# A hybrid decoder layer: GpSimd's stores issued two steps later in the forgetting stage

## The chip, the cores and the metric

The kernel runs on one core of a Trainium2 chip. A core has TensorE (matrix products, PE in the profile), VectorE (DVE), ScalarE (ACT), GpSimd (POOL) and SyncE (SP), each with a queue of its own that it works off in order, and 16 DMA engines that all queues share. The time is microseconds on the device for one execution; less is better.

## The reference

One decoder layer with two groups of attention heads over the same input (2048 rows, width 1024).

```python
h = rms_norm(x, g_pre) * (1 + scale) + shift          # shift, scale, gate from silu(c) @ w_ada + b_ada
qa, ka, va, fa, za, qb, kb, vb, zb = split(h @ w_in)
# A, "forgetting": causal softmax attention, 8 heads of 64, with a bias cum[q] - cum[k],
#    cum = cumsum(log_sigmoid(fa + b_fgate)) over the rows
oa = forgetting_attention(qa, ka, va, fa + b_fgate) * silu(za)
# B: sliding window of 128 with sinks, 8 query heads, 2 key heads, rotary positions
ob = sliding_window_sink_attention(rope(qb), rope(kb), vb, sinks) * silu(zb)
y = concatenate([oa, ob]) @ w_out
x + gate * rms_norm(y, g_post)
```

The change touches group A's stage, in which three more things are done on the side: gate paths `silu(za)`, the projection of the next heads' queries and keys, and the vector `gate * g_post`, with `gate = silu(c) @ w_ada[:, 2048:] + b_ada[2048:]`.

## The kernel before

The order of instructions on each engine is written out by hand (`tc.manual_schedule()`), so an engine's queue follows the order in which the Python code runs. Waits between engines are set by the tiles that they share.

**Stages.** Opening and normalisation, then projections with the sliding window (to about 485 us in the profile), the forgetting stage, and the output projection. In the forgetting stage a loop runs over 160 *steps*: 8 heads of 20 steps, and step `s` is `hd, r = divmod(s, 20)`. A step takes two blocks of 128 keys against up to 512 queries:

- `scores`: TensorE writes the scores into the PSUM tile `sta` (L1248, L1249), of which there is one.
- `exp32`: ScalarE takes the exponential into `p` (L1253). In the steps on the diagonal, r = 0, 1, 4, 5, 10, 11, 18 and 19, GpSimd then applies the causal mask to `p` in place (L1257, `affine_select`).
- `high`: ScalarE copies `p` to f16 in `pha` (L1261), after the mask where there is one.
- `low`: VectorE takes the rest, `p` minus that copy (L1264), one step later.
- `pv`: TensorE multiplies both with the values (L1274 to L1277), two steps later.

So on ScalarE the next step's exponential stands behind this step's `high`, and the next scores but one can be written only when that exponential has read `sta`.

**Between them** `todo`, a list of small units, is spread over each step: one unit of a projection (L305) for the heads ahead (through `fill`), or one matmul that finds row maxima of the scores (L1199), which VectorE reduces (L1202, L1204). `events` hang a weight's preparation on the counts of these units: `w_load` loads a weight of 512 KB (L203), `w_max` reduces it on VectorE to a maximum per partition (L209) and stores that to DRAM (`mx_d`, L212), `w_back` loads all 128 of them back to every partition (`mxr`, L217), `w_scale` takes their maximum (L228) and sets the scale, `w_high` and `w_low` split the weight. All DMAs of this list are issued from GpSimd's queue, the one that applies the masks.

**Delays.** `after(n, f)` calls `f` at the n-th `tick()` from then, and there are two ticks in a step. `evac_z` takes a finished gate path out of PSUM this way: ScalarE's tanh after one tick (L349), VectorE's product after two (L345), and with it the store of the tile `tz` to `z_d` (L347, 256 KB) from GpSimd. There are two tiles `tz`.

**The residual gate.** `gate_load(k)` loads rows of `w_ada` into the one tile `gw` (512 KB, L1128, from GpSimd), for k = 0 to 9 at the end of step 8k; `gate_use(k)` accumulates them in `gacc` on VectorE (L1134) at the end of step 8k + 6.

Of the kernel before, what the change touches and what calls it, by code (L numbers as in the profile page):

```python
# [21 lines left out]
KT = D // P  # L22
# [18 lines left out]
def hybrid_layer(  # L41
# [17 lines left out]
    V, A, G, PE, SP = nc.vector, nc.scalar, nc.gpsimd, nc.tensor, nc.sync  # L59
# [20 lines left out]
    def sm(n, tag):  # L80
        return small.tile([P, n], F32, tag=tag, name=tag)
# [98 lines left out]


    late = []

    def after(n, f):
        late.append([n, f])

    def tick():
        now = [f for n, f in late if n <= 1]
        late[:] = [[n - 1, f] for n, f in late if n > 1]
        for f in now:  # L190
            f()


    wq = {}
# [12 lines left out]
    def w_max(key):  # L207
        mx = sm(1, "w_mx")
        V.tensor_reduce(mx[:], wq[key][0][:], axis=AX.XY, op=ALU.max, apply_absolute_value=True)  # L209
        md = mx_d[len(kaps_seen) % 3]  # L210
        kaps_seen.append(key)
        G.dma_start(md[:], mx[:])  # L212
        wq[key].append(md)

    def w_back(key):
        mxr = mxp.tile([P, P], F32, tag="mxr", name="mxr")
# [123 lines left out]
    def evac_z(kt, key, ci):  # L340
        def evac(ps, free):
            t = op_.tile([P, CH], F32, tag="tz", name="tz")

            def mul():
                V.scalar_tensor_tensor(t[:], t[:], 1.0, ps, op0=ALU.add, op1=ALU.mult)  # L345
                free()
                G.dma_start(z_d[kt, :, ci * CH:(ci + 1) * CH], t[:])  # L347

            after(1, lambda: A.activation(t[:], ps, AF.Tanh, scale=czs[key][:]))  # L349
            after(2, mul)  # L350

        return evac
# [557 lines left out]
    for kind, j in (("zb", 0), ("zb", 1), ("va", 0), ("zb", 2), ("zb", 3), ("va", 1), ("va", 2)):  # L910
        key = f"{kind}{j}"
# [104 lines left out]
    def fill(n, each=None):  # L1016

        for _ in range(n):
            for f in events.pop(pos[0], []):
                f()  # L1020
            punits[pos[0]]()
            pos[0] += 1
            if each:
                each()
# [3 lines left out]
    def tick2():  # L1028
        cnt[0] += 1
        if cnt[0] % 2 == 0:  # L1030
            tick()
# [113 lines left out]
    def const_rows(n, slot):  # L1145

        px = bk[bank()][:]
        PE.matmul(px[0:XR, 0:P], fx["cst"][:, slot // 2, :], identh[:], start=True, stop=True)
        for c_ in range(NCH):
            after(1, lambda c_=c_: A.activation(  # L1150
                Ts[n][64:XR, slot, c_ * CH:(c_ + 1) * CH].rearrange("p (u q) -> p u q", u=4),
                px[64:XR, 0:P].unsqueeze(1).broadcast_to([XR - 64, 4, P]), AF.Copy))
# [18 lines left out]
    def key_limbs(hd):  # L1171

        cv = sm(NB, "a_cv")
        V.tensor_scalar(cv[:], csum[:, hd, :], isc[f"qk{hd}"][:], None, op0=ALU.mult)
        for col, x_, nx in ((0, XA, True), (1, XB, True), (2, XC, False)):
            V.tensor_scalar(lk[:, col, :], cv[:], 1.0 / x_, None, op0=ALU.mult)
            if nx:
                cv2 = sm(NB, "a_cv")
                V.scalar_tensor_tensor(cv2[:], lk[:, col, :], -x_, cv[:], op0=ALU.mult, op1=ALU.add)
                cv = cv2  # L1180

    def key_rows(hd):
        T = Ts[hd % 2]
        ext_rows(lk[:].rearrange("p r b -> p (r b)"), 3 * NB,
                 [(0, 2 * NB, T[64:66, 2, :]), (2 * NB, NB, T[68:69, 2, :])])
# [145 lines left out]
    def w_out_load(m):  # L1331
        k, cc = m % KT, slice((m // KT) * CH, (m // KT + 1) * CH)
        w_raw[m] = stp.tile([P, CH], F32, tag="st", name=f"wo{m}")
        SP.dma_start(w_raw[m][:], w_out0[k * P:(k + 1) * P, cc])

    def w_out_split(m):
        k, cc = m % KT, slice((m // KT) * CH, (m // KT + 1) * CH)
        raw, hi = w_raw.pop(m), w_slot(k)[:, cc]
        A.activation(hi, raw[:], AF.Copy, scale=wsc[:, k:k + 1])
        V.scalar_tensor_tensor(w_slot(8 + k)[:, cc], raw[:], wsc[:, k:k + 1], hi, op0=ALU.mult, op1=ALU.subtract)  # L1340
# [3 lines left out]
    class Out:  # L1344
# [85 lines left out]
        def store(self):  # L1430
            y, rst = self.y, self.rst
            parts = 2 if self.t == NB - 1 else 1
            for n in range(parts):
                cc = slice(n * D // parts, (n + 1) * D // parts)
                V.scalar_tensor_tensor(y[:, cc], y[:, cc], rst[:], self.x[:, cc], op0=ALU.mult, op1=ALU.add)  # L1435
                SP.dma_start(os_[self.t * P:(self.t + 1) * P, cc], y[:, cc])
# [15 lines left out]
    def ofill(n, each=None):  # L1452
        for _ in range(n):
            if opos[0] in oloads:
                outs[oloads[opos[0]]].load()
            ounits[opos[0]]()
            opos[0] += 1
            if each:
                each()

    with tc.manual_schedule():
        mi = 0
        V.memset(cmask[:], 0.0)
        V.tensor_copy(cmask[:, 3 * P:], dmask[:])
        for n in range(2):
            for slot in (2, 0):
                const_rows(n, slot)
                tick()
        fill(8, tick2)
        key_limbs(0)  # L1470
        key_rows(0)
        tick()
        while pos[0] < N_V3 or mi < M_LEAD:
            if pos[0] < N_V3:
                fill(1)
            if mi < M_LEAD and pos[0] >= N_QK0 - 10:
                munits[mi]()
                mi += 1
            tick2()
        for _ in range(3):  # L1480
            tick()
        steps[0].scores()
        p0, p_tot = pos[0], len(punits) - pos[0]

        w_at = {2: [0], 3: [1], 4: [2], 5: [3], 6: [4], 8: [5], 10: [6], 11: [7], 12: [8], 13: [9], 14: [10],
                15: [11, 12], 16: [13, 14], 17: [15]}
        w_all = sum(s.w for s in steps[:7 * NS])
        w_acc = 0
        for s, stp_ in enumerate(steps):
            hd, r = divmod(s, NS)  # L1490
            w_acc += stp_.w
            npn = p0 + min(p_tot, 14 + p_tot * w_acc // w_all) - pos[0]
            fil = fill
            if hd == 7 and r >= 8:
                npn, fil = N_IN * max(r - 9, 0) // (NS - 10) - opos[0], ofill
            m_goal = min(len(munits), M_LEAD + int(round((s + 1) * M_HEAD / NS)))
            todo = []
            nmn = m_goal - mi
            a = b = 0
            while a < npn or b < nmn:  # L1500
                if b >= nmn or (a < npn and a * nmn <= b * npn):
                    todo.append(lambda: fil(1))
                    a += 1
                else:
                    todo.append(munits[mi + b])
                    b += 1
            mi = m_goal
            half = (len(todo) + 1) // 2
            if r == 2 and hd + 1 < 8:
                key_limbs(hd + 1)  # L1510
            if hd == 7 and r:
                for m in w_at.get(r + 3, []):
                    w_out_load(m)
            stp_.exp32()
            tick()
            if s:
                steps[s - 1].low()
            if hd == 7:
                for m in w_at.get(r, []):
                    w_out_split(m)  # L1520
            for u in todo[:half]:
                u()
            stp_.high()
            if s + 1 < len(steps):
                steps[s + 1].scores()
            tick()
            if s >= PV_LAG:
                steps[s - PV_LAG].pv()
            for u in todo[half:]:
                u()  # L1530
            if r == 3 and hd + 1 < 8:
                key_rows(hd + 1)
            if hd == 7 and r == 0:
                open_out()
            if hd == 7 and r == 0:
                for m in w_at[2] + w_at[3]:
                    w_out_load(m)
            if hd == 7 and r in (4, 6):
                outs[r // 2 - 2].load()
            if hd == 7 and r in (6, 8):  # L1540
                outs[r // 2 - 3].turn(4)
            if s % 8 == 0 and s // 8 < KT + 2:
                gate_load(s // 8)
            if s % 8 == 6 and s // 8 < KT + 2:
                gate_use(s // 8)
        assert pos[0] == len(punits) and mi == len(munits) and opos[0] == N_IN and not events
        tick()
        steps[-1].low()
        for n in range(PV_LAG, 0, -1):
            steps[-n].pv()  # L1550
        tick()
        tick()
        fxs.close()
        ofill(len(ounits) - opos[0], tick2)
        for _ in range(4):
            tick()
# [34 lines left out]
```

## Time and profile before

| what | value |
|---|---|
| median of 3 runs | 1225.0 us (1220.46 to 1227.03) |
| the profiled execution | 1220.06 us, its span 1218.4 us |
| granted TensorE clock, mean | 0.985 |
| PE busy | 1158.1 us, 95% of the span |
| DVE, ACT, POOL busy | 908.6, 672.6, 177.3 us |
| forgetting stage, steps 0 to 159 | about 485 to 1050 us |

The times of single instructions are from one execution. A row of the timeline has the start in us from the span's first instruction, the duration in us, the engine, the line of the source, the operation, the tile written and the tiles read, and in brackets how long the engine had been idle and what ended that. A row of waits has who waited for whom: us in total, times, the longest. A row of stages has, after its limits and its length, each engine's busy time with its number of instructions, then TensorE's granted clock, the DMA engines' busy share and GB/s. "POOL L1257" is the causal mask, "POOL L212" the store of maxima, "POOL L217" their load, "POOL L347" the store of a gate path, "POOL L1128" the residual gate's load.

### The profile page before, as it was taken

The numbers are of one execution on the slowest core, as the hardware profiler recorded it, in microseconds if no ns is written. First come the engines' busy times: TensorE is split into PE (matmuls) and PEld (weight loads), VectorE is DVE, ScalarE is ACT, GpSimd is POOL, SyncE is SP. The second block draws the span as 40 slices with busy tenths as digits, with TensorE's granted clock in tenths as the row PEclk, the third lists the DMA queues.
The fourth block names the chain that finished last, engine by engine and source line by source line (L and its number), as shares of the span: only waits on it lengthen the run. The fifth ranks groups of instructions, "written<-read, shape, count | busy, mean of one in ns | idle before, by whom it ended". The sixth has DMA issues, their size and how long they took to land. (4 is left out here: it accounts for less than half of the span.)

```text
span 1218.4 us, 27236 instructions
## 1 busy us (share of the span) xinstructions
PE 1158.1 (95%) x10704; PEld 689.3 (57%) x10704; DVE 908.6 (75%) x2267; ACT 672.6 (55%) x1116; POOL 177.3 (15%) x315
## 2 busy tenths in 40 slices
PE   6789999999999999998999999999999979999997
PEld 2457546865558966554555555555555545555553
DVE  6866567586776647687888799878978797676665
ACT  2766445555655442565666666666766778333231
POOL 2011133223232210111111111021000000000000
PEclk9899999999999999998999999999999999999999
DMA  9554333324323322322225322123111136446652
GB/s 324 188 146 139 83 94 73 86 55 103 94 72 83 57 60 45 82 62 79 67 75 74 92 66 70 43 63 61 37 43 46 56 115 191 143 155 191 196 169 84
DMA packets 88036, 120.70 MB, mean 99 GB/s; under 512 B 27836, under 2 KB 63716, under 8 KB 87908
## 3 DMA queue, kind: packets, MB, share of 16 engines
q1 hardware_dynamic: 76932, 85.94, 23.8%
q0 software_dynamic: 10976, 33.03, 11.7%
q8 instruction: 84, 1.38, 0.6%
q14 instruction: 44, 0.36, 0.1%
HBM read 71.56 MB, written 25.18 MB: 79 GB/s over the span
## 5 line engine op out<-in xcount | busy, mean ns | idle before, releaser
L1253 ACT ACTIVATE p<-sta,lift,scl_qk 128x1024 f32<-128x1024 f32 (+2 forms) x160 | 171.7, 1073 | 104.3 <-PE sta L1249 97.1
L305 PE MATMUL bk<-hT,wh_qk 128*128 128x512 f16 x768 | 196.0, 380 | 0.9 <-DVE a_m L1202 0.9
L1261 ACT ACTIVATE pha<-p 128x1024 f16<-128x1024 f32 (+2 forms) x160 | 148.1, 926 | 50.4 <-POOL p L1257 38.6
L1399 PE MATMUL bk<-wohl,oz 128*128 128x512 f16 x768 | 172.4, 379 | 2.2 <-DVE oz L1386 1.0
L1202 DVE TENSOR_REDUCE a_m<-bk 128x1 f32<-128x512 f32 x192 | 130.2, 685 | 53.4 <-PE bk L1199 52.6
L1264 DVE TENSOR_TENSOR pha<-p,pha 128x1024 f16<-128x1024 f32 (+2 forms) x160 | 169.4, 1059 | 0.2 <-ACT pha L1261 0.2
L1399 PEld LDWEIGHTS <-oz 128*128 128x128 f16 x768 | 74.4, 99 | 84.2 <-issue 1.8
L1274 PE MATMUL poa<-vt,pha 128*128 128x65 f16 x1088 | 117.9, 194 | 2.6 <-DVE ona L1283 2.6
L1248 PE MATMUL sta<-T 128*128 128x512 f16 (+1 forms) x320 | 110.6, 351 | 9.7 <-ACT p L1253 9.6
L1277 PE MATMUL poa<-vt,pha 128*128 128x65 f16 x1088 | 117.5, 193 | 1.3 <-DVE pha L1264 1.3
L1276 PE MATMUL poa<-vt,pha 128*128 128x64 f16 x1088 | 117.8, 195 | 0.0
L305 PEld LDWEIGHTS <-wh_qk 128*128 128x128 f16 x768 | 72.8, 98 | 76.7 <-issue 3.3
L1199 PE MATMUL bk<-T 66*128 66x512 f16 (+2 forms) x320 | 110.3, 351 | 2.1 <-DMA T<-stq 1.9
L1274 PEld LDWEIGHTS <-pha 128*128 128x128 f16 x1088 | 102.4, 97 | 17.2 <-DVE ona L1283 3.4
L1276 PEld LDWEIGHTS <-pha 128*128 128x128 f16 x1088 | 101.9, 98 | 13.7 <-issue 0.3
L1249 PE MATMUL sta<-T 69*128 69x512 f16 (+1 forms) x320 | 108.8, 350 | 0.0
L1277 PEld LDWEIGHTS <-pha 128*128 128x128 f16 x1088 | 101.7, 99 | 1.6 <-DVE pha L1264 1.6
L305 PE MATMUL bk<-hT,wh_za 128*128 128x512 f16 x384 | 99.8, 378 | 0.0
L323 PE MATMUL bk<-wh_va,hT 128*128 128x128 f16 x1536 | 91.0, 219 | 1.0 <-issue 1.0
L323 PEld LDWEIGHTS <-hT 128*128 128x128 f16 x1536 | 87.5, 98 | 6.2 <-issue 3.5
L305 PE MATMUL bk<-hT,wh_zb 128*128 128x512 f16 x384 | 89.9, 379 | 1.1 <-DVE wh_zb L249 1.1
L305 PE MATMUL bk<-hT,wh_qb 128*128 128x512 f16 x384 | 87.2, 379 | 0.0
(487 smaller groups left out, 1881.2 us busy)
## 6 DMA issues: line engine op xcount, KB each, us to landing
wa<-in_w_ada_dram SPq DMA_DIRECT2D x16, 512.0 KB
z_d<-tz POOLq DMA_DIRECT2D x32, 256.0 KB, 2.9
T<-stq SPq DMA_DIRECT2D x128, 64.0 KB
T<-o_d SPq DMA_DIRECT2D x16, 512.0 KB
T<-z_d SPq DMA_DIRECT2D x16, 512.0 KB
xr<-in_x_dram SPq DMA_DIRECT2D x16, 512.0 KB
out_dram<-yg SPq DMA_DIRECT2D x15, 512.0 KB
xt<-in_x_dram SPq DMA_DIRECT2D x12, 512.0 KB
```

What stands on the lines that cost most here:

```text
L305: PE.matmul(ps, whl[:, a, k, :], hT[ci][:, b, k, :], start=(k == 0 and n == 0), stop=(k == KT - 1 and n == 2))
L323: PE.matmul(ps[:, u * P:(u + 1) * P], hT[ci][:, a, k, u * P:(u + 1) * P], whl[:, b, k, :], start=(k == 0 and n == 0), stop=(k == KT - 1 an ...
L1199: PE.matmul(mx[:, :w], T[0:XM, 0, i * P:(i + 1) * P], T[0:XM, 2, pc * CH:pc * CH + w], start=True, stop=True)
L1202: V.tensor_reduce(m3[:, u, pc:pc + 1], mx[:, :w], axis=AX.X, op=ALU.max)
L1248: PE.matmul(self.st[:, o:o + w], T[:, 3, kb_], T[:, 1, qc], start=True, stop=False)
L1253: A.activation(self.p32[:, :self.w], self.st[:, :self.w], AF.Exp, scale=scl[f"qk{self.hd}"][:], bias=lift[:])
L1261: A.activation(self.ph[:, 0, :self.w], self.p32[:, :self.w], AF.Copy)
L1264: V.tensor_tensor(self.ph[:, 1, :self.w], self.p32[:, :self.w], self.ph[:, 0, :self.w], op=ALU.subtract)
L1274: PE.matmul(po[:, u, :], ph[:, 0, pq], vt[:, b, hd, 0:65], start=(self.first and n == 0 and u == 0), stop=False)
L1276: PE.matmul(po[:, u, 0:64], ph[:, 0, pq], vt[:, b, hd, 65:VW], start=False, stop=False)
L1277: PE.matmul(po[:, u, :], ph[:, 1, pq], vt[:, b, hd, 0:65], start=False, stop=(self.last and n == len(self.blocks) - 1))
L1399: PE.matmul(py, self.hl[:, i, k, :], w_slot(8 * j + k)[:, cc], start=(k == 0 and m_ == 0), stop=(k == KT - 1 and m_ == 2))
```

## The change

Three things, all in the forgetting stage. From the loop's start on `lag[0]` is 4, which is four ticks or two steps: by so much later `w_max` issues its store of maxima, and `evac_z` its store of a gate path (after the product). The reduction and the product stay where they are. `gate_load(k)` moves to the end of step 8k + 2, and `gate_use(k)` to the end of step 8k + 7.

```diff
     late = []
+    lag = [0]
...
         md = mx_d[len(kaps_seen) % 3]
         kaps_seen.append(key)
-        G.dma_start(md[:], mx[:])
-        wq[key].append(md)
+
+        def put():
+            G.dma_start(md[:], mx[:])
+            wq[key].append(md)
+
+        if lag[0]:
+            after(lag[0], put)
+        else:
+            put()
...
             def mul():
                 V.scalar_tensor_tensor(t[:], t[:], 1.0, ps, op0=ALU.add, op1=ALU.mult)
                 free()
+                if lag[0]:
+                    after(lag[0], store)
+                else:
+                    store()
+
+            def store():
                 G.dma_start(z_d[kt, :, ci * CH:(ci + 1) * CH], t[:])
...
         w_acc = 0
+        lag[0] = 4
         for s, stp_ in enumerate(steps):
...
-            if s % 8 == 0 and s // 8 < KT + 2:
+            if s % 8 == 2 and s // 8 < KT + 2:
                 gate_load(s // 8)
-            if s % 8 == 6 and s // 8 < KT + 2:
+            if s % 8 == 7 and s // 8 < KT + 2:
                 gate_use(s // 8)
```

What it does to the queues is seen at three places. Line numbers of the changed kernel are up to 14 higher.

GpSimd's queue from step 16 to step 25, before. The masks (AFFINE_SELECT) are those of steps 18, 19, 20, 21, 24 and 25; `mx_d_74` and `mx_d_75` hold the maxima of the weights qk3 and za1.

```order
L1128 DMA gw_8004<-in_w_ada_dram 128x1024
L1257 AFFINE_SELECT p_8061<-p_8061 128x2x128
L1257 AFFINE_SELECT p_8109<-p_8109 128x2x128
L1257 AFFINE_SELECT p_8159<-p_8159 128x2x128
L212 DMA mx_d_74<-w_mx 128x1
L212 DMA mx_d_75<-w_mx 128x1
L1257 AFFINE_SELECT p_8214<-p_8214 128x2x128
L1257 AFFINE_SELECT p_8346<-p_8346 128x2x128
L217 DMA mxr<-mx_d_74 128x128
L217 DMA mxr<-mx_d_75 128x128
L1128 DMA gw_8408<-in_w_ada_dram 128x1024
L1257 AFFINE_SELECT p_8410<-p_8410 128x2x128
```

The same part of GpSimd's queue in the changed kernel:

```order
L1271 AFFINE_SELECT p_8059<-p_8059 128x2x128
L1142 DMA gw_8107<-in_w_ada_dram 128x1024
L1271 AFFINE_SELECT p_8109<-p_8109 128x2x128
L1271 AFFINE_SELECT p_8159<-p_8159 128x2x128
L1271 AFFINE_SELECT p_8212<-p_8212 128x2x128
L215 DMA mx_d_74<-w_mx 128x1
L215 DMA mx_d_75<-w_mx 128x1
L1271 AFFINE_SELECT p_8346<-p_8346 128x2x128
L225 DMA mxr<-mx_d_74 128x128
L225 DMA mxr<-mx_d_75 128x128
L1271 AFFINE_SELECT p_8408<-p_8408 128x2x128
L1142 DMA gw_8495<-in_w_ada_dram 128x1024
```

The two stores of maxima have passed behind the mask of step 21, the loads of the residual gate behind the masks of steps 18 and 25. The loads `mxr` stand where they stood.

GpSimd's queue from step 96 to step 101, before: the maxima of qk7 and za3, with the masks of steps 98, 99, 100 and 101.

```order
L212 DMA mx_d_74<-w_mx 128x1
L212 DMA mx_d_75<-w_mx 128x1
L1257 AFFINE_SELECT p_12126<-p_12126 128x2x128
L1257 AFFINE_SELECT p_12175<-p_12175 128x2x128
L1257 AFFINE_SELECT p_12230<-p_12230 128x2x128
L217 DMA mxr<-mx_d_74 128x128
L217 DMA mxr<-mx_d_75 128x128
L1257 AFFINE_SELECT p_12280<-p_12280 128x2x128
```

And in the changed kernel:

```order
L1271 AFFINE_SELECT p_12124<-p_12124 128x2x128
L215 DMA mx_d_74<-w_mx 128x1
L215 DMA mx_d_75<-w_mx 128x1
L1271 AFFINE_SELECT p_12175<-p_12175 128x2x128
L1271 AFFINE_SELECT p_12230<-p_12230 128x2x128
L225 DMA mxr<-mx_d_74 128x128
L225 DMA mxr<-mx_d_75 128x128
L1271 AFFINE_SELECT p_12280<-p_12280 128x2x128
```

The stores have passed behind one mask, that of step 98, and two masks are left between them and the loads.

VectorE's queue in steps 22 and 23, before (`gacc` is the residual gate's accumulation, `pha` the `low` of steps 22 and 23):

```order
L1134 SCALAR_TENSOR_TENSOR gacc<-gw_8004,sil,gacc 128x1024
L1264 TENSOR_TENSOR pha<-p_8257,pha 128x1024
L1202 TENSOR_REDUCE a_m<-bk_6615 128x1
L1281 RECIPROCAL a_ri<-poa 128x4
L1283 TENSOR_TENSOR ona<-poa,a_ri 128x256
L1204 ISA bk_133,a_m<-bk_133,cmask 128x256
L1204 ISA a_m 128x1
L980 SCALAR_TENSOR_TENSOR stq<-bk_134,stq 128x512
L1264 TENSOR_TENSOR pha<-p_8305,pha 128x1024
```

And in the changed kernel:

```order
L1278 TENSOR_TENSOR pha<-p_8255,pha 128x1024
L1216 TENSOR_REDUCE a_m<-bk_6615 128x1
L1295 RECIPROCAL a_ri<-poa 128x4
L1297 TENSOR_TENSOR ona<-poa,a_ri 128x256
L1218 ISA bk_133,a_m<-bk_133,cmask 128x256
L1218 ISA a_m 128x1
L1148 SCALAR_TENSOR_TENSOR gacc<-gw_8107,sil,gacc 128x1024
L994 SCALAR_TENSOR_TENSOR stq<-bk_134,stq 128x512
L1278 TENSOR_TENSOR pha<-p_8304,pha 128x1024
```

The accumulation has gone from ahead of the `low` of step 22 to ahead of that of step 23.

## The prediction, made before the changed kernel had run

> **What bounds the kernel now.** I read the page's first line and its row of busy times, then the stages, then TensorE's waits in the stage that the diff touches, then the instructions of four engines around the longest of those waits.
>
> ```profile
> span 1218.4 us, 27236 instructions
> PE 1158.1 (95%) x10704; PEld 689.3 (57%) x10704; DVE 908.6 (75%) x2267; ACT 672.6 (55%) x1116; POOL 177.3 (15%) x315
> ...
> core 0: us, PE busy (x) PEld busy (x) DVE busy (x) ACT busy (x) POOL busy (x), PEclk, DMA share, GB/s
> 485.00:970.00 485.00, 479.44 (x4645) 266.29 (x4643) 400.53 (x884) 311.61 (x362) 65.09 (x112) 0.99 0.26 62
> 970.00:1050.00 80.00, 68.02 (x771) 42.06 (x770) 67.60 (x130) 63.31 (x83) 7.02 (x11) 0.96 0.42 129
> ...
> PE sta L1248 <- ACT p L1253: 4.4, 4, 3.2
> PE bk L305 <- DVE a_m L1202: 0.9, 1, 0.9
> ```
>
> The forgetting stage runs from 485 us. Up to 970 us TensorE is busy 479.44 of 485.00 us, so whatever the change does there, TensorE can give back at most the 5.56 us that it idles, and what a lowered clock costs beside that. The two waits (TensorE's waits in 485 to 970) hold nearly all of it: 4.4 us in four waits of the scores' matmul (L1248) for the exponential (L1253), 3.2 of it in one. After 970 us there is more idle time, but the order there is not changed except for two stores. The long wait, engine by engine (start, duration, instruction, idle before it and what ended that):
>
> ```profile
> 567.23 0.58 POOL L212 DMA_DIRECT2D mx_d<-w_mx  x1 [4.17 <-DVE w_mx L209]
> 568.35 0.55 POOL L212 DMA_DIRECT2D mx_d<-w_mx  x1 [0.55 <-DVE w_mx L209]
> 568.90 1.15 POOL L1257 TENSOR_SCALAR_AFFINE_SELECT p<-p 128x256 f32<-128x256 f32 x1
> ...
> 565.72 1.21 DVE L209 TENSOR_REDUCE w_mx<-wr_qk 128x1 f32<-128x1024 f32 x1
> 566.85 1.21 DVE L209 TENSOR_REDUCE w_mx<-wr_za 128x1 f32<-128x1024 f32 x1
> ...
> 563.95 0.65 ACT L1253 ACTIVATE p<-sta,lift,scl_qk 128x384 f32<-128x384 f32 x1
> 570.09 0.52 ACT L1261 ACTIVATE pha<-p 128x384 f16<-128x384 f32 x1 [5.48 <-POOL p L1257]
> 570.67 1.18 ACT L1253 ACTIVATE p<-sta,lift,scl_qk 128x1024 f32<-128x1024 f32 x1
> ...
> 571.90 0.58 PE L1248 MATMUL sta<-T 128*128 128x512 f16 x1 [3.21 <-ACT p L1253]
> ```
>
> This is step 21. Its exponential ended at 564.60, but its causal mask on GpSimd (L1257) began only at 568.90: ahead of it in GpSimd's queue stood two stores of weight maxima, which waited for VectorE's reductions (the second ends at 568.06). ScalarE's copy (L1261) waited 5.48 us for the mask, the next exponential stood behind that copy, and TensorE's next scores waited 3.21 us for the one scores tile. Then comes what the gap did to the clock:
>
> ```profile
> 565.00:571.35 6.35, 3.69 (x26) 1.60 (x24) 6.25 (x12) 1.26 (x3) 2.27 (x3) 1.00 0.14 31
> 571.35:578.17 6.82, 6.26 (x34) 2.95 (x34) 3.10 (x10) 3.82 (x4) 0.00 (x0) 0.50 0.08 20
> 578.17:590.00 11.83, 11.83 (x120) 6.67 (x119) 9.73 (x17) 6.59 (x9) 2.38 (x5) 1.00 0.46 102
> sum 25.00, PE 21.79 PEld 11.22 DVE 19.08 ACT 11.68 POOL 4.65; mean PE 7.26 PEld 3.74 DVE 6.36 ACT 3.89 POOL 1.55
> ```
>
> (PEclk, third from the right, is TensorE's granted clock.) It is 0.50 from 571.35 to 578.17, so 6.26 us of matmuls cost 3.13 us more than at full clock. The stall is worth 3.21 + 3.13 = 6.34 us.
>
> **The change, part by part.** *The nine stores of maxima* (weights qk2 to qk7, za1 to za3) are issued two steps after their reduction. GpSimd still runs ahead: what counts is which masks stand between. At step 21 the mask now stands first, and the wait for VectorE falls after it. The 6.34 us go. Two more places have the same pattern:
>
> ```profile
> 640.04 0.42 POOL L1257 TENSOR_SCALAR_AFFINE_SELECT p<-p 128x256 f32<-128x256 f32 x1
> 642.05 0.38 PE L1248 MATMUL sta<-T 128*128 128x512 f16 x1 [0.15 <-ACT p L1253]
> 706.75 0.42 POOL L1257 TENSOR_SCALAR_AFFINE_SELECT p<-p 128x256 f32<-128x256 f32 x1
> 708.76 0.27 PE L1248 MATMUL sta<-T 128*128 128x256 f16 x1 [0.71 <-ACT p L1253]
> 817.31 0.61 POOL L1257 TENSOR_SCALAR_AFFINE_SELECT p<-p 128x256 f32<-128x256 f32 x1
> 817.96 0.52 ACT L1261 ACTIVATE pha<-p 128x384 f16<-128x384 f32 x1 [2.46 <-POOL p L1257]
> ```
>
> Masks without idle time of GpSimd before them came straight from behind a store. At 640.04 (step 40) and 706.75 (step 59) TensorE then idled 0.15 and 0.71 us; these go too.
>
> *The sixteen stores of gate paths.* Their wait for VectorE's product held masks as well, the worst at 817.31 (step 91), where ScalarE waited 2.46 us. But TensorE has no wait there: two steps of lag between a copy and its use cover it. I take 0 for this part. Its own risk is the tile `tz`, of which there are two, freed later by the later store:
>
> ```profile
> z_d<-tz POOLq DMA_DIRECT2D x32, 256.0 KB, 2.9
> 953.44 0.40 POOL L1257 TENSOR_SCALAR_AFFINE_SELECT p<-p 128x256 f32<-128x256 f32 x1 [2.63 <-ACT p L1253]
> 970.39 0.54 POOL L347 DMA_DIRECT2D z_d<-tz  x1 [11.43 <-DVE a_m L1204]
> ```
>
> The tightest reuse is the last path (stored at 970.39), which takes the tile of the path two before it. That one's store now follows the mask at 953.44 and lands 2.9 us after its issue, near 957.4, some ten microseconds ahead of need: 0.
>
> *The residual gate's ten loads and ten accumulations.* Loads move from residue 0 to 2 of eight steps, accumulations from 6 to 7. The load comes three steps after the accumulation that frees its tile instead of two, so it waits less, not more. Ahead of a mask it costs its issue:
>
> ```profile
> 582.59 0.54 POOL L1128 DMA_DIRECT2D gw<-in_w_ada_dram  x1
> 577.77 1.28 DVE L1134 SCALAR_TENSOR_TENSOR gacc<-gw,sil,gacc 128x1024 f32<-128x1024 f32 x1
> ```
>
> 0.54 us of issue fits in the idle time that GpSimd has before nearly every mask: 0. The accumulation's 1.28 us only changes its place on VectorE. That matters where VectorE is short of time, and this is the stretch of step 21: VectorE has 19.08 us of work in the 25.00 us above, and TensorE without the stall wants 25.00 - 6.34 = 18.66. So VectorE is over by 0.42 us. Between 0 (two steps of lag take it up) and 1.28 (the accumulation stands in front of a `low` that TensorE wants) I take 0.42, the row's own difference.
>
> *What is late next: the maxima's way back.* The broadcast load (L217) waits on GpSimd until the store has landed, and masks queue behind it. It keeps its place, while the store comes later:
>
> ```profile
> mx_d<-w_mx POOLq DMA_DIRECT2D x23, 0.5 KB, 7.6
> 706.20 0.55 POOL L212 DMA_DIRECT2D mx_d<-w_mx  x1 [0.54 <-DVE w_mx L209]
> 714.31 0.54 POOL L217 DMA_DIRECT2D mxr<-mx_d  x1 [1.18 <-DMA mx_d<-w_mx]
> 583.89 0.40 POOL L1257 TENSOR_SCALAR_AFFINE_SELECT p<-p 128x256 f32<-128x256 f32 x1 [0.76 <-ACT p L1253]
> 841.48 1.02 POOL L1257 TENSOR_SCALAR_AFFINE_SELECT p<-p 128x256 f32<-128x256 f32 x1
> 848.39 0.41 POOL L1257 TENSOR_SCALAR_AFFINE_SELECT p<-p 128x256 f32<-128x256 f32 x1 [3.23 <-ACT p L1253]
> 850.72 0.40 POOL L1257 TENSOR_SCALAR_AFFINE_SELECT p<-p 128x256 f32<-128x256 f32 x1 [0.73 <-ACT p L1253]
> ```
>
> From the start of such a store to the start of the load that waited for it pass 714.31 - 706.20 = 8.11 us. For qk7 and za3 the two stores now follow the mask at 841.48 (ended 842.50), so the second starts near 843.1, the second load near 851.2, done near 851.7; the mask of step 101, wanted at 850.72, is 1.0 us late. At step 25 (stores start at 567.23 and 568.35 as now) the second load ends near 568.35 + 8.11 + 0.55 = 577.0, and the mask, at 583.89 before, is wanted at 583.89 - 6.34 = 577.5: no delay. The price lies between 0 and the row where lateness first shows: a mask 1.8 us late (step 91) cost TensorE nothing, one 2.1 us late 0.15. I take 0, nearest to 1.0.
>
> [...]
>
> **Sum.** 3.21 + 3.13 + 0.15 + 0.71 - 0.42 = 6.78 us. The profiled execution took 1220.06 us (span 1218.4), which becomes 1213.3. It is one of the quicker ones, 4.9 us under the median of 1225.0 (runs from 1220.46 to 1227.03); the saving is the same stretch of program in all of them, so against the median I forecast 1225.0 - 6.8 = 1218.2.
>
> **Rivals.** *Only the idle time comes back.* Halved clock begins and ends on steps of 3.41 us (6.82 is two of them), so how many a gap costs may differ between executions. Without the clock's part the gain is 6.78 - 3.13 = 3.65: 1221.4. For it: the gap was 3.21 us, shorter than one such step. Against: the profile shows the drop right behind it.
>
> [...]
>
> *More than the sum.* The median lies 4.9 us above the profiled run; if part of that is further half-clock steps behind the same gap, or if the other waits of the stage (0.9 us of the row for L305) go with it, 2 to 4 us more: 1215.
>
> *The stall comes back at the maxima's load, and the kernel is slower.* Place: GpSimd before the masks of steps 25 and 101. A mask 4.30 us late cost 6.34 us at step 21. For step 25 that needs a store that takes 8.1 + 0.5 + 4.3 = 12.9 us instead of 8.1, for step 101 8.1 - 1.0 + 4.3 = 11.4. One such stall cancels the gain (1224.6), two make 1225.0 - 6.8 + 12.7 = 1230.9. It decides from about 12 us on; the longest seen is a good 8.
>
> *It does nothing*: VectorE, busy 6.25 of the 6.35 us before 571.35, keeps the pace even without the queue, and TensorE waits for its reductions instead. Gain under 1 us: 1224.5. Against: from 571.35 on it was idle for more than half, so it waited for TensorE.
>
> **Chances.** Forecast (1216 to 1221) 0.58, more than the sum 0.10, idle time alone 0.16, nothing 0.10, stall back 0.06. Bounds: 1212 is the forecast less 1.3 for the other waits and less the 4.5 us by which runs fall below the median; 1224.5 is the idle-only case with 1.28 for VectorE in place of 0.42, plus the 2.0 us by which they rise. 0.5%, about what this measurement can tell from no change, is 6.1 us, so the border is 1218.9, close above the forecast: six tenths of the forecast's case and all of the second are faster (0.45), rounded to 0.48 because the slower runs have more to lose; same 0.46, slower 0.06.
>
> **What the profile after would show.** The mask of step 21 starts some 0.1 us after its exponential, no 3.21 us wait of L1248, granted clock 1.00 from 485 to 970. The masks of steps 40, 59 and 91 have idle time before them. The stores of maxima have no wait for L209 where masks follow. The loads L217 do wait for the stores. I am wrong if a mask behind L217 starts more than 2 us after its exponential, if L1202 or `low` holds TensorE near step 23, or if the clock still drops there.

## The result, and the profile after

The changed kernel took 1215.34 us (median of 5 runs, 1214.56 to 1216.32), the kernel before 1225.0 us beside it (1220.46 to 1228.74): a ratio of 0.9921, 95% interval 0.9894 to 0.9947. In a later session, beside the last of the experiments, the same two kernels took 1213.62 and 1219.11 us: 0.9957, interval 0.9945 to 0.9969, which is 3.8 to 6.7 us. So it is faster, by 5.5 us where it was measured most closely and 9.7 us in the first session.

The profiled execution took 1216.32 us. First the page's first line and TensorE's row, then the stage up to 970 us:

```profile
span 1214.5 us, 27231 instructions
PE 1159.6 (95%) x10704; PEld 690.9 (57%) x10704; DVE 909.5 (75%) x2267; ACT 673.4 (55%) x1116; POOL 175.0 (14%) x315
```

```profile
core 0: us, PE busy (x) PEld busy (x) DVE busy (x) ACT busy (x) POOL busy (x), PEclk, DMA share, GB/s
485.00:970.00 485.00, 483.10 (x4743) 270.27 (x4740) 406.48 (x896) 316.43 (x366) 63.90 (x113) 1.00 0.27 63
```

TensorE now idles 1.90 us of these 485 instead of 5.56, at a granted clock of 1.00. All that is left of its waits from 485 to 965 us:

```profile
PE poa L1288 <- DVE ona L1297: 0.7, 1, 0.7
PE sta L1262 <- ACT p L1267: 0.4, 1, 0.4
PE poa L1291 <- DVE pha L1278: 0.2, 1, 0.2
```

The waits of the scores for the exponential, 4.4 us in four before, are one of 0.4. Step 21, engine by engine (the mask is now L1271, the store of maxima L215):

```profile
567.28 0.66 ACT L1267 ACTIVATE p<-sta,lift,scl_qk 128x384 f32<-128x384 f32 x1
...
568.01 0.80 POOL L1271 TENSOR_SCALAR_AFFINE_SELECT p<-p 128x256 f32<-128x256 f32 x1 [1.61 <-ACT p L1267]
570.57 0.56 POOL L215 DMA_DIRECT2D mx_d<-w_mx  x1 [1.76 <-DVE w_mx L210]
571.69 0.54 POOL L215 DMA_DIRECT2D mx_d<-w_mx  x1 [0.56 <-DVE w_mx L210]
...
568.84 0.52 ACT L1275 ACTIVATE pha<-p 128x384 f16<-128x384 f32 x1 [0.90 <-POOL p L1271]
...
573.60 0.21 PE L1288 MATMUL poa<-vt,pha 128*128 128x65 f16 x1 [0.70 <-DVE ona L1297]
```

Late means from the end of a step's exponential to the start of its mask. The mask is first in the queue and 0.07 us late instead of 4.30; the two stores wait for VectorE behind it, and the next mask (step 24, at 578.99) comes long after them. What is left is 0.70 us in which TensorE waits for VectorE, which has the two reductions of maxima in this step as before.

The profiles are best compared by stretches. Between the exponentials of two steps the time is the same in all executions to about 0.1 us, but for what differs in the kernels and for the clock. The table gives the time from the start of one step's exponential to that of another, in us, for the ten profiles of this study.

| kernel | 20 to 30 | 38 to 44 | 56 to 64 | 64 to 84 | 96 to 104 | 0 to 138 |
|---|---|---|---|---|---|---|
| before | 41.42 | 19.90 | 27.54 | 71.42 | 27.30 | 488.0 |
| before, again | 41.28 | 19.90 | 27.52 | 71.44 | 27.30 | 487.9 |
| stores of gate paths only | 38.42 | 19.89 | 27.51 | 71.43 | 27.30 | 485.0 |
| residual gate only | 38.41 | 19.70 | 30.38 | 70.79 | 27.31 | 487.0 |
| change without the pair | 41.41 | 19.70 | 26.66 | 70.79 | 27.31 | 486.3 |
| pair only | 36.52 | 19.91 | 27.52 | 71.33 | 27.30 | 483.0 |
| all maxima, nothing else | 36.51 | 19.70 | 26.66 | 71.56 | 27.30 | 482.2 |
| change | 35.92 | 19.70 | 26.66 | 70.79 | 27.30 | 480.8 |
| change, again | 35.92 | 19.69 | 26.65 | 70.79 | 27.30 | 480.8 |
| maxima three steps later | 35.93 | 19.70 | 26.66 | 70.79 | 29.09 | 482.6 |

From step 0 to step 138 the change gains 488.0 - 480.8 = 7.2 us against the first profile of before. The spans differ by only 3.9 us: ahead of step 0, where nothing was changed, the profiled execution of the changed kernel took 489.0 us and that of before 485.6; its second profile took 486.5. That stage varies by itself: over the ten profiles it took from 484.2 to 489.0 us, a scatter almost as large as the gain.

### The profile page after: what moved, and what is told of

Its sections match the earlier page's. It is cut to its first block, busy times and chain, and to the rows that moved or that the text cites. A ratio compares the mean times of both kernels' runs of the same rounds, so it can differ in the third digit from the quotient of the medians.

```text
span 1214.5 us, 27231 instructions
## 1 busy us (share of the span) xinstructions
PE 1159.6 (95%) x10704; PEld 690.9 (57%) x10704; DVE 909.5 (75%) x2267; ACT 673.4 (55%) x1116; POOL 175.0 (14%) x315
## 3 DMA queue, kind: packets, MB, share of 16 engines
HBM read 71.56 MB, written 25.18 MB: 80 GB/s over the span
## 5 line engine op out<-in xcount | busy, mean ns | idle before, releaser
L1271 POOL TENSOR_SCALAR_AFFINE_SELECT p<-p 128x256 f32<-128x256 f32 x64 | 32.6, 509 | 414.2 <-ACT p L1267 409.4
```

## The experiments

**The three parts alone.** From the changed kernel, only the lag of `w_max` kept:

```diff
-                if lag[0]:
-                    after(lag[0], store)
-                else:
-                    store()
+                store()
...
-            if s % 8 == 2 and s // 8 < KT + 2:
+            if s % 8 == 0 and s // 8 < KT + 2:
...
-            if s % 8 == 7 and s // 8 < KT + 2:
+            if s % 8 == 6 and s // 8 < KT + 2:
```

> The kernel before, with only the stores of maxima issued two steps later; gate paths, residual gate as before. Queue theory (the gain is the wait of the masks behind the stores of maxima, above all at step 21, and the median of before lies higher than its profile because that wait costs more in other executions): all of the change's gain, ratio about 0.992 to before (1215 to 1217 us), no mask over 1 us late behind a store of maxima. Spread theory (the stores of gate paths or the gate's loads give what the sum of 6.8 us lacks of the measured 9.7): ratio 0.9945, 1218 us.

Measured: 1213.41 us against 1218.72, ratio 0.9954 (0.9941 to 0.9967). That is within the interval of the whole change (0.9957, from another session on another chip): the stores of maxima carry it. The medians can't tell whether they give all of it. By the stretches of the traces they give 488.0 - 482.2 = 5.8 us of the change's 7.2. The number 0.992 was not reached, by this or by the whole change in the later session. What this kernel still has between steps 20 and 30 are two waits of TensorE for VectorE, of which the change has only the first:

```profile
PE poa L1285 <- DVE ona L1294: 0.7, 1, 0.7
PE bk L1210 <- DVE a_m L1213: 0.4, 1, 0.4
```

Only the lag of `evac_z` kept (and the gate's loads and accumulations back at residues 0 and 6, as above):

```diff
-        if lag[0]:
-            after(lag[0], put)
-        else:
-            put()
+        put()
```

> The kernel before, with only the stores of gate paths issued two steps later. Queue theory: no change (ratio 0.999 to 1.001), the 3.2 us gap at step 21 is still there, the masks of steps 91 and 104 are no longer late. Spread theory: 2 to 3 us faster, ratio 0.998.

Measured: 1219.83 us, ratio 1.0005 (0.9993 to 1.0017): nothing. The masks of steps 91 and 104 are no longer late, and the stretch from 84 to 96 stays at 41.95 us: the two steps of lag had covered them. This profile shows something else. It has the same gap at step 21:

```profile
570.55 0.38 PE L1259 MATMUL sta<-T 128*128 128x512 f16 x1 [3.21 <-ACT p L1264]
```

But the clock behind it is not halved (three stretches of 3.41 us along the clock's own steps, the granted clock third from the right):

```profile
565.67:569.08 3.41, 1.67 (x12) 0.67 (x8) 3.38 (x6) 0.35 (x1) 2.25 (x3) 1.00 0.03 3
569.08:572.49 3.41, 1.94 (x27) 1.23 (x27) 2.26 (x11) 3.35 (x5) 0.00 (x0) 1.00 0.15 39
572.49:575.91 3.42, 3.42 (x26) 1.82 (x25) 3.17 (x4) 2.27 (x4) 0.00 (x0) 1.00 0.00 0
```

The gap lies half in one of these windows and half in the next, 1.74 and 1.47 us. Steps 20 to 30 take 38.42 us instead of 41.42.

Only the residual gate moved, both lags out (the two lines take the place of the choices by `lag[0]`):

```diff
+        put()
...
+                store()
```

> The kernel before, with only the residual gate's loads and accumulations moved. Queue theory: no change (ratio 0.999 to 1.001), the gap at step 21 is there. Spread theory: 1 to 3 us faster. The accumulation one step later may also change the 0.91 us wait of TensorE near 747 us; that alone is too little to measure.

Measured: 1220.60 us, ratio 1.0013 (1.0000 to 1.0026): not faster, if anything a little slower. The gap at step 21 is there, again without a halved clock (38.41 us from step 20 to 30). Its trace at step 59 shows a place where it loses:

```profile
700.47 0.58 POOL L215 DMA_DIRECT2D mx_d<-w_mx  x1 [4.10 <-DVE w_mx L210]
701.59 0.56 POOL L215 DMA_DIRECT2D mx_d<-w_mx  x1 [0.53 <-DVE w_mx L210]
702.14 0.54 POOL L1136 DMA_DIRECT2D gw<-in_w_ada_dram  x1
702.68 1.13 POOL L1265 TENSOR_SCALAR_AFFINE_SELECT p<-p 128x256 f32<-128x256 f32 x1
...
705.41 0.30 PE L1256 MATMUL sta<-T 128*128 128x256 f16 x1 [1.96 <-ACT p L1261]
```

```profile
702.10:705.51 3.41, 1.45 (x8) 0.58 (x6) 3.27 (x9) 1.51 (x2) 1.73 (x4) 1.00 0.97 16
705.51:708.92 3.41, 3.41 (x30) 2.24 (x29) 2.56 (x5) 2.03 (x3) 0.79 (x2) 0.50 0.90 47
```

The load's issue of 0.54 us now stands between the blocked stores and the mask of step 59. The mask is 4.23 us late instead of 3.70, it takes 1.13 us instead of 0.42, TensorE's gap grows from 0.71 to 1.96, and in this execution it also halves the clock: 30.38 us from step 56 to 64 instead of 27.54. With the stores of maxima out of the way, the same load costs nothing (26.66, with the load moved or not).

**The pair of step 20.** The change, with the stores for qk3 and za1 issued at once again:

```diff
-        if lag[0]:
+        if lag[0] and key not in ("qk3", "za1"):
             after(lag[0], put)
```

> The changed kernel, but the two stores of maxima of step 20 (weights qk3 and za1) are issued at once again. Queue theory: the stall of step 21 comes back with its clock, 6.3 us or more: 1221.5 to 1225, ratio to before 0.997 to 1.000, a mask about 4 us late and a granted clock of 0.5 behind it. Rival (VectorE or the phase of the clock set the gain, and the pair was one of many small delays): under 3 us lost, at most 1218.

Measured: 1216.49 us, ratio 0.9982 (0.9972 to 0.9992). The stall is back, the mask 4.30 us late as in the kernel before:

```profile
567.53 0.56 POOL L215 DMA_DIRECT2D mx_d<-w_mx  x1 [4.17 <-DVE w_mx L210]
568.66 0.54 POOL L215 DMA_DIRECT2D mx_d<-w_mx  x1 [0.56 <-DVE w_mx L210]
569.21 1.15 POOL L1271 TENSOR_SCALAR_AFFINE_SELECT p<-p 128x256 f32<-128x256 f32 x1
...
572.21 0.59 PE L1262 MATMUL sta<-T 128*128 128x512 f16 x1 [3.21 <-ACT p L1267]
```

```profile
568.24:571.65 3.41, 0.76 (x5) 0.24 (x3) 3.31 (x9) 1.26 (x3) 1.69 (x2) 1.00 0.01 0
571.65:578.48 6.83, 6.27 (x34) 2.96 (x34) 3.12 (x10) 3.83 (x4) 0.00 (x0) 0.50 0.08 20
```

In this execution 2.65 us of the gap lie in one window, and the clock is halved for the next two. In the trace the pair is worth 41.41 - 35.92 = 5.5 us. In the medians, against the change in the other session, it is 0.9982 - 0.9957, about 3 us. The ratio lies in what was expected. The absolute time does not, since the whole session ran some 6 us quicker than the first, and neither the 3 us nor the time tells the queue theory from its rival (under 3 us lost, at most 1218). The trace does: the rival has no place for a stall that comes back whole with these two stores. The 6.3 us expected at the least were too many, as the price of the stall is 5.5 in the trace.

And the other way round, the kernel before with only these two stores delayed:

```diff
-        if lag[0]:
+        if lag[0] and key in ("qk3", "za1"):
             after(lag[0], put)
```

> The kernel before, with only the two stores of step 20 (weights qk3 and za1) issued two steps later; all other stores as before. Phase theory: steps 20 to 30 take 36 to 36.5 us instead of 38.4 or 41.4, steps 56 to 64 stay at 27.5; 2 to 5 us faster than before, ratio 0.996 to 0.998. With the complement (the change without this pair, 0.998) it makes up the whole change's ratio. Rival (the pair's stall only moves on to VectorE's backlog): under 1 us.

Measured: 1214.53 us, ratio 0.9967 (0.9957 to 0.9976). Two stores out of the 35 instructions that the change moves on GpSimd give more than half of the gain, 488.0 - 483.0 = 5.0 us of 7.2 in the traces; with the complement (0.9982) it makes 0.9949, the whole change 0.9957, within the intervals.

**Both kernels again**, unaltered, in the same session as the run just told and the one that follows:

> The changed kernel unaltered, against before in the same session as the parts. Phase theory (the stretches of the forgetting stage are the same to 0.1 us in each execution, apart from the halved clock behind a gap, which comes or not by phase: steps 20 to 30 took 41.4 or 38.4 us with the same 3.2 us gap): steps 20 to 30 take 35.9 and steps 0 to 138 take 480.8 us again; gain over before in the median between 4.2 (no drop) and 7.2 us (drop always), about 5.5 to 6.0, ratio 0.995 to 0.996. Rival (the 9.7 us of the first session are the change's own worth, from something that its one profile of before did not show): ratio 0.992 again.

> The kernel before, unaltered, for a second profile of it. Phase theory: steps 20 to 30 take 41.4 or 38.4 us, nothing between but 39.7 to 39.9 (one of two steps of halved clock); every other stretch of the forgetting stage up to step 138 as in the first profile within 0.1 us, but for a drop at step 59 (27.5, or up to 30 us from step 56 to 64). Rival (before loses more elsewhere in other executions): another stretch is longer by over 1 us.

Measured: the change 0.9957 (0.9945 to 0.9969), 5.5 us, as the phase theory had it; before against itself 1.0001 (0.9990 to 1.0012). The stretches came as expected, steps 20 to 30 of before with 41.28 us where 41.4 was named. In the five profiles that have the gap at step 21 (before twice, gate paths only, residual gate only, the change without the pair) the clock was halved behind it in three. Worked out from that, the change should gain 4.2 us without a drop (485.0 - 480.8) and 7.2 with it, 6.0 at three in five; 5.5 was measured, with an interval (3.8 to 6.7) that can't tell these shares apart. Both profiles of the kernel before itself have the drop; the two without it are of variants. The 9.7 us of the first session are not explained by this: its runs of before lie 6 us over those of the later sessions, those of the change 2 us. Which stretch was longer in them no profile shows, and it stays open.

**The way back of the maxima.** The change, with the stores of maxima a further step later:

```diff
         if lag[0]:
-            after(lag[0], put)
+            after(lag[0] + 2, put)
```

> The changed kernel, with the stores of maxima issued three steps later instead of two; the rest as in the change. Way-back theory (a store takes about 8 us to its load, and masks queue behind the load): the stores for qk7 and za3 come behind the mask of step 99 and the mask of step 101 is 3.2 to 3.6 us late, TensorE idles 0.5 to 2.5 us there and may lose the clock's 1.7 us as well; steps 96 to 104 take 27.8 to 31 us instead of 27.3; 0.5 to 4 us slower than the change. [...]

Measured: 1214.31 us, ratio to before 0.9965 (0.9951 to 0.9978), where the change has 0.9957; the difference of 0.7 us in the medians lies within the intervals. The medians do not decide on the way-back theory; the trace does. GpSimd at steps 99 to 101 and TensorE's wait behind:

```profile
838.73 1.13 POOL L215 DMA_DIRECT2D mx_d<-w_mx  x2
841.93 0.40 POOL L1271 TENSOR_SCALAR_AFFINE_SELECT p<-p 128x256 f32<-128x256 f32 x1 [2.07 <-ACT p L1267]
846.87 1.09 POOL L225 DMA_DIRECT2D mxr<-mx_d  x2 [4.54 <-issue]
847.97 0.42 POOL L1271 TENSOR_SCALAR_AFFINE_SELECT p<-p 128x256 f32<-128x256 f32 x1
...
850.24 0.38 PE L1262 MATMUL sta<-T 128*128 128x512 f16 x1 [1.63 <-ACT p L1267]
```

```profile
848.46:851.87 3.41, 1.78 (x27) 1.14 (x26) 2.49 (x11) 3.35 (x5) 0.00 (x0) 1.00 0.61 73
851.87:855.28 3.41, 3.41 (x24) 1.61 (x20) 2.87 (x4) 2.27 (x3) 0.00 (x0) 1.00 0.04 11
```

From the stores to the loads pass 846.87 - 838.73 = 8.1 us. The row of the loads names no releaser for the 4.54 us before them, but in this stage of the profiles before and after, wherever such a row does name the store's landing, 7.5 to 8.9 us lie between (from 705.08 to 712.57 us before, from 510.03 to 518.93 after). The mask of step 101 is 3.79 us late (3.2 to 3.6 expected), TensorE idles 1.63 us, and steps 96 to 104 take 29.09 us instead of 27.30. The way back takes over the role that the stores had before. In the change itself the same place shows how near it is:

```profile
838.57 1.13 POOL L215 DMA_DIRECT2D mx_d<-w_mx  x2
846.21 1.09 POOL L225 DMA_DIRECT2D mxr<-mx_d  x2 [1.29 <-DMA mx_d<-w_mx]
847.30 0.42 POOL L1271 TENSOR_SCALAR_AFFINE_SELECT p<-p 128x256 f32<-128x256 f32 x1
```

The mask starts right at the end of the loads' issue, 0.53 us after its exponential; TensorE does not notice.

## Why the prediction was right, and where it was off

The forecast was 1218.2 us and 6.8 us gained; measured were 9.7 us in its own session and 5.5 in the later one. That the number lies between the two is partly luck: 1215.34 us is outside the forecast's own case (1216 to 1221) and on that of the rival *More than the sum* (1215), of whose two sources only the wait of L305 is seen to go, with 0.6 us. And the step from the profile to the median failed: the saving is not the same in all executions (4.2 us without the drop of the clock, 7.2 with it), and the 1225.0 us of three runs did not come back (1218.72 and 1219.11 in the later sessions). The mechanism was right: the stores of maxima held the mask of step 21, and taking them out of its way carries the gain. Term by term, by the stretches of the first two profiles:

- *The stall of step 21* was put at 3.21 + 3.13 = 6.34 us, less 0.42 for VectorE. Measured: 41.42 - 35.92 = 5.50. Two terms were mis-sized. VectorE's is 0.70 us instead of 0.42, inside its bounds of 0 and 1.28: the wait for `ona` (L1297), where the prediction looked at L1202 and `low`. The clock's is 41.42 - 38.42 = 3.00 instead of 3.13. So 3.21 + 3.00 - 0.70 = 5.51.
- *The clock's 3.13 us* were counted as if each execution had them. Three of five profiles do. So "only the idle time comes back" was less a rival to the forecast than a part of its executions, two of five profiles here. The row that spoke against it (0.50 behind the gap) was one execution. That the gap was shorter than one step of 3.41 us decided nothing: where 2.65 us of it lay in one window of that length the clock was halved (the change without the pair), where 1.74 and 1.47 us lay in two it was not (stores of gate paths only).
- *Steps 40 and 59* were put at 0.15 + 0.71 and gave 0.20 + 0.88.
- *The gate paths* were put at 0: they gave 0.
- *The residual gate's move* was put at 0 beside VectorE's term. With the maxima moved alone, the accumulation's 1.28 us stand on VectorE ahead of the reduction for which TensorE waits another 0.4 us in steps 20 to 30 (L1210); in the change that wait is gone, and the stretch is 0.6 us shorter (36.51 to 35.92). No run has the maxima and the gate without the gate paths, so that this is the gate's work is read from VectorE's queue. It gives 0.6 to 0.8 in 64 to 84, where the wait of L305 for VectorE's reduction is gone. Alone it loses 2.8 us in one execution at step 59. "0.54 us of issue fits in the idle time" holds only where the queue ahead of it does not stand.
- *The way back*: a mask 1.0 us late at step 101 and none at step 25, TensorE untouched. Measured: 0.53 and 0.07 us, TensorE untouched. A store takes 7.6 to 8.1 us to its load in these rows. The place that the rival named for step 101 is a real one: with one step more of delay the mask is 3.79 us late and TensorE idles 1.63 us. Its price of 6.34 us, and so its limit of 11.4 us for a store, were not put to the test.
- *The signs.* All came but one: the stores of maxima still wait for VectorE (1.76 us at step 21), only no mask stands close behind them now.
- *The upper bound* of 1224.5 us comes to 1224.3 by its own terms, 1221.4 + 0.86 + 2.0.

The sum by the stretches, 5.50 + 0.20 + 0.88 + 0.63 = 7.2 us, is close to the forecast's 6.8. The gain of the medians in the later session is 1.3 us under the forecast; that the clock's part is not always there would account for it, but is not shown execution by execution.

## What to carry to other kernels

In a queue that issues DMAs and also does short work on the critical chain, a DMA that has to wait should not stand in front of that work: look for critical instructions that have no idle time before them, and ask what stood ahead. A delay counts only where nothing covers it: a mask 4.30 us late cost 5.5 us here where the clock was halved behind it, one 1.81 us late nothing. Moving the waiting DMA behind the next critical instruction was enough here, but its reader in the same queue must be moved with it or have a store's whole time (7.5 to 8.9 us here) between. And the gap of 3.2 us at step 21 cost its length in five profiles and in three of them some 3 us of halved clock besides (41.28 to 41.42 us from step 20 to 30, against 38.41 and 38.42): take several profiles before counting a clock drop as a gap's price.

## What the runs showed of the hardware that was not expected

In all ten profiles, cut from 120 to 1205 us into windows of 3.41 us, the granted clock is 1.00 or 0.50 in a whole window, and each profile has its own grid: the first window starts at 120.79 us in the profile of before and at 123.37 in its second. There are 40 windows at 0.50. With each window's length less TensorE's busy time as its idle time, each of the 20 full-clock windows with 1.94 us of it or more was followed by a half-clock window, and none of those with less than 1.36 us; between 1.36 and 1.86 us ten were and twelve were not. There the sum alone did not tell which, nor was one piece needed: in the run with the maxima three steps later, pieces of 1.02 and 0.35 us in one window were followed by half clock (the window from 981.58 us), and in the profile of before 1.68 us of a single gap of 1.93 were not (the window from 458.71 us). The gap of 3.2 us at step 21 cost some 3 us of clock where it left 2.40 to 2.66 us of idle time in one window (before twice, the change without the pair), and none where it was split into 1.74 and 1.47 us (stores of gate paths only) or 1.69 and 1.52 us (residual gate only).

A store of 128 single values of four bytes to DRAM took 7.5 to 8.9 us to the load that waited for it (profiles before and after, this stage). By the page of before, the median of such a store from issue to landing is 7.6 us, and that of one of 256 KB on the same queue 2.9.
